# The state-space scan's 248 small operations, issued on GpSimd in place of VectorE

## The chip, the cores and the metric

The kernel runs on one core of a Trainium2 chip. The metric is the device time of one execution in microseconds (us). In the profile, PE is TensorE (matmul) and PEld its weight loads, DVE is VectorE, ACT is ScalarE, POOL is GpSimd, and SP is SyncE, which issues most DMAs. The span is the time from the first to the last instruction of the one execution that was profiled.

## The reference

The reference is one encoder layer over 512 tokens of width 1024. Two mixers run side by side, a state-space branch (S5) and a gated spatial branch (SGU), are merged by sigmoid gates, and are followed by cross-attention on 256 memory tokens and a SwiGLU network of width 2816. The part that matters here is the S5 branch:

```python
def s5_scan(u, lam_re, lam_im, log_step, b_re, b_im, c_re, c_im, reverse):
    ...
    lam_bar = jnp.exp(lam * step)
    ...
    bu = jnp.einsum('gpc,lbgc->lbgp', b_bar, u.astype(jnp.complex64))
    a = jnp.broadcast_to(lam_bar[None, None], (seq, 1) + lam_bar.shape)
    _, states = lax.associative_scan(_linear_recurrence, (a, bu), axis=0, reverse=reverse)
    ...
    return jnp.einsum('gcp,lbgp->lbgc', c, states).real

def s5_branch(xa, ...):
    ...
    for direction, reverse in ((0, False), (1, True)):
        y = y + s5_scan(...)
    y = jax.nn.gelu(y.transpose(1, 0, 2, 3).reshape(bsz, seq, S5_WIDTH))
    y = y * jax.nn.sigmoid(y @ w_glu.astype(f32))
    return y.astype(xa.dtype)
```

There are 32 groups of 64 complex states, and one scan forward and one backward over the 512 positions.

## The kernel before, in words

**Tiles and products.** All weights are float32. A product of float32 matrices is made of three passes (`mm3`): each operand is split into a high part `hi`, a cast to a shorter format on ScalarE (L85), and a low part `lo`, a subtraction on VectorE (L86). A block of weights (128 x 1024 elements) is loaded by SyncE into `wraw`, cast into `whi`, and subtracted into `wlo`. `next_w` begins loads three blocks ahead and splits two blocks ahead; `whi` and `wlo` have three buffers each. One block of `feat` is 24 matmuls of 512 columns.

**Order.** The kernel is written as one sequence, and a planner (`TileContext(nc, schedule_with_timeline_sim=True)`) orders the instructions of every engine before the run, by its own times and by the program's order. What `in_order` pins comes behind all that was written before it on its engine; what follows may still be put ahead of it. On the chip every engine takes its queue in order.

**The side program.** The S5 branch is a generator that runs beside the main sequence of products. Each `yield` names the time that the instructions since the last one are worth. `tick(us)`, called after each piece of TensorE work, gives the generator a credit of 0.8 of that time, and resumes it for as long as there is credit; `later(n, fn)` puts a piece of work n ticks of 5.2 us later. A `yield` also decides how far down the main sequence the following S5 work is written. `finish_side`, behind the product 6 of the second half of `w_proj_b`, writes whatever is left.

**The scan.** Sequence positions are taken in 64 chunks of 8. The state inputs of all chunks are in `zh` (128 partitions: 64 states forward and 64 backward; free: chunk, real and imaginary part, 32 groups). `s5_inputs` fills `zh` (matmuls `pz` L968, copies L973 on ScalarE and L974 on VectorE). `s5_scan` then goes through chunks 1 to 62, with four operations on 128 x 64 elements for each: two products with the constants `ca` and `cb` (L996, L997), and two additions (L998, L999). Each chunk needs the one before.

**After the scan.** For each of four parts o of eight groups, `s5_outputs` sets two edges of `ss` to zero on GpSimd (L1010, L1011), copies the states out of `zh`, one half on ScalarE (L1012) and one on VectorE (L1013), multiplies on TensorE (`py` L1025), copies (`yn` L1034), turns on TensorE (`pyt` L1040), and copies into `y` (L1045). Parts 2 and 3 must first load their factors again (`reload`, L943 and L936). `store_outputs`, called at three places between the products of `w_proj_b` and once behind `finish_side`, takes the parts that are there by then: a GELU on ScalarE (L1057) and two DMAs on GpSimd (`yd`, L1060). Then `ygt` is read back (L1366), split (L1372, L1373), and the GLU's product begins on TensorE.

**The main sequence beside it.** In this order: `feat` blocks of the gates a (`ga0` to `ga3`, two blocks each), `psv` (L1214), the blocks of `zu`, the gates b (`gb0` to `gb3`, L1289), and the products of `w_proj_b` in seven half-size products for each half of the columns: 1, 5, 2, 6 of the first half, 1 of the second, 7, 2 (second), 4, 6 (second); `finish_side`; then 3, 7, 5, 4, 3 and the GLU.

**GpSimd's other work.** It raises norms to a power (L1153, L516), and issues DMAs: `kd` (L921), and the additions onto `bsum`, `qsum` and `dsum` (L294), each behind a first DMA that SyncE issues (L293).

Of the kernel before, what the change touches and what calls it, by code (L numbers as in the profile page):

```python
# [12 lines left out]
ALU = mybir.AluOpType  # L13
# [39 lines left out]
def hybrid_layer_kernel(  # L53
# [8 lines left out]
    nc = tc.nc  # L62
# [630 lines left out]
    st = {}  # L693
    V = nc.vector
# [294 lines left out]
            later(1, lambda i=i, e=e: turn(i, e))  # L989

    def s5_scan():
        zh = st["zh"]
        for n in range(1, NCH - 1):
            a = s5p.tile([P, 2, G], F32, tag="sa", name="sa", bufs=2)
            b = s5p.tile([P, 2, G], F32, tag="sb", name="sb", bufs=2)
            V.tensor_tensor(a, zh[:, n - 1], st["ca"], ALU.mult)  # L996
            V.tensor_tensor(b, zh[:, n - 1, ::-1, :], st["cb"], ALU.mult)  # L997
            V.tensor_tensor(a, a, zh[:, n], ALU.add)  # L998
            V.tensor_tensor(zh[:, n], a, b, ALU.add)  # L999
            yield 0.8  # L1000

    def s5_outputs(o):
        gs = slice(o * GO, (o + 1) * GO)
# [58 lines left out]
    def s5_program():  # L1062
        yield from s5_setup()
        for o in (2, 3):
            yield from s5_kernels(o)
        while "u" not in st:
            yield None
        zh = s5p.tile([P, NCH, 2, G], F32, name="zh")
        st["zh"] = zh
        for o in range(NO):  # L1070
            yield from s5_inputs(o)
        for o in (0, 1):
            yield from s5_kernels(o)
        while st.get("nz", 0) < 2 * NO:
            yield None
        yield None
        yield from s5_scan()
        for _ in range(2):
            yield None
        for o in range(NO):  # L1080
            yield from s5_outputs(o)
# [949 lines left out]
```

## Time and profile before

| | |
|---|---|
| time, median of two runs | 861.31 us (860.77 to 861.85) |
| span of the profiled execution | 859.5 us |
| TensorE busy | 852.2 us, 99% |
| VectorE busy | 663.7 us, 77% |
| ScalarE busy | 465.9 us, 54% |
| GpSimd busy | 86.2 us, 10%, 119 instructions |
| chain that ended last | TensorE 98% |
| scan, first and last operation | 135.0 and 227.8 us |

The profiled execution's own time is its span, 859.5 us, and what lies around it; the median of the runs is 1.8 us above the span. A row of the timeline has the start, the duration, the engine, the line, the operation, what is written from what is read, the shapes, and in square brackets how long the engine was idle before it and what ended that. A row of the groups has a count, the busy time, the mean of one in ns, and the idle time before them. The rows of the waits have the total, the number of times and the longest one in us.

### The profile page before, as it was taken

What the parts mean: (1) busy time and instruction counts of PE and PEld (TensorE: products, weight loads), DVE (VectorE), ACT (ScalarE), POOL (GpSimd) and SP (SyncE); (2) the same over time, 40 slices, a digit from 0 to 9 for tenths busy, and PEclk for the clock granted to TensorE, in tenths of its full rate; (3) what the DMA queues carried; (4) which work ended last, traced back from release to release, by engine and by line L of the source; (5) the groups of instructions that cost most, each with busy time, mean ns of one, the idle gap of its engine ahead of it and who ended that gap; (6) DMA issues with size and microseconds to landing.
All of it is one profiled execution on the core that took longest, in us unless ns stands there. A gap on an engine that the chain in (4) does not pass through costs nothing.

```text
span 859.5 us, 14730 instructions
## 1 busy us (share of the span) xinstructions
PE 852.2 (99%) x5760; PEld 764.1 (89%) x5760; DVE 663.7 (77%) x1078; ACT 465.9 (54%) x698; POOL 86.2 (10%) x119
## 2 busy tenths in 40 slices
PE   9999999999999999999999999999999999999997
PEld 6888888888889988899899888999999999988886
DVE  7898898899646867678758656767877768899776
ACT  7834953244455534457557444645545554655674
POOL 0002101211021111010010001010211111000000
PEclk9999999999999999999999999999999999999999
DMA  9869666888575798635696555557899898366664
GB/s 270 229 229 252 143 171 160 227 212 203 138 221 162 250 321 260 213 110 196 215 275 169 133 152 143 147 176 180 206 242 234 209 230 219 96 186 203 200 192 164
DMA packets 116200, 170.61 MB, mean 198 GB/s; under 512 B 9489, under 2 KB 80801, under 8 KB 116002
## 3 DMA queue, kind: packets, MB, share of 16 engines
q1 hardware_dynamic: 95778, 140.51, 50.8%
q0 software_dynamic: 20064, 28.55, 20.3%
q8 instruction: 45, 0.74, 0.3%
q10 hardware_dynamic: 288, 0.61, 0.2%
q14 instruction: 25, 0.20, 0.1%
HBM read 160.75 MB, written 48.73 MB: 244 GB/s over the span
## 4 chain that ended last, share of the span: by engine, by line
PE 98%; DMA 1%; ACT 0%; SPq 0%; DVE 0%; issue 0%
PE pf L379 27%; PE pt L379 17%; PE px L1261 13%; PE pq L1261 6%; PE dx L379 5%; PE dq L379 5%; PE pv L1261 3%; PE bx L1261 3%; PE qx L1261 3%; PE dv L379 2%; PE pz L968 2%; PE qv L1261 1%; PE po L379 1%; PE psc L379 1%; PE py L1025 1%; PE qq L1261 1%
## 5 line engine op out<-in xcount | busy, mean ns | idle before, releaser
L85 ACT CAST whi<-wraw 128x1024 fp32r<-128x1024 f32 x141 | 145.3, 1031 | 161.4 <-PE pf L379 61.0
L86 DVE TENSOR_TENSOR wlo<-wraw,whi 128x1024 fp32r<-128x1024 f32 x141 | 168.2, 1195 | 55.5 <-ACT whi L85 54.8
L379 PE MATMUL pf<-xn,whi 128*128 128x512 f32 x448 | 139.4, 392 | 0.0
L379 PEld LDWEIGHTS pf<-xn,whi 128*128 128x128 f32 x448 | 83.4, 188 | 16.9 <-issue 0.2
L379 PE MATMUL pf<-xn,wlo 128*128 128x512 f32 x224 | 87.7, 392 | 0.0
L1261 PE MATMUL px<-fn,whi 128*128 128x256 f32 x480 | 83.5, 277 | 0.0
L1261 PEld LDWEIGHTS px<-fn,whi 128*128 128x128 f32 x480 | 72.5, 188 | 0.2
L86 DVE TENSOR_TENSOR wlo<-b,whi 128x1024 fp32r<-128x1024 f32 x40 | 48.9, 1223 | 26.0 <-ACT whi L85 26.0
L85 ACT CAST whi<-b 128x1024 fp32r<-128x1024 f32 x40 | 42.2, 1054 | 47.8 <-PE px L1261 27.8
L1261 PE MATMUL px<-fn,wlo 128*128 128x256 f32 x240 | 66.4, 277 | 0.0
L1261 PE MATMUL pq<-s,whi 128*128 128x256 f32 x320 | 55.0, 276 | 0.0
L86 DVE TENSOR_TENSOR wlo<-t,whi 128x1024 fp32r<-128x1024 f32 x30 | 36.7, 1225 | 19.4 <-ACT whi L85 19.4
L85 ACT CAST whi<-t 128x1024 fp32r<-128x1024 f32 x30 | 31.6, 1054 | 36.1 <-PE pv L1261 13.4
L379 PEld LDWEIGHTS pf<-xn,wlo 128*128 128x128 f32 x224 | 42.0, 188 | 8.9 <-issue 0.2
L1261 PEld LDWEIGHTS pq<-s,whi 128*128 128x128 f32 x320 | 48.1, 188 | 0.0
L1261 PEld LDWEIGHTS px<-fn,wlo 128*128 128x128 f32 x240 | 45.1, 188 | 0.0
L1261 PE MATMUL pq<-s,wlo 128*128 128x256 f32 x160 | 44.2, 276 | 0.0
L379 PE MATMUL pt<-whi,xn 128*128 128x512 f32 x128 | 43.4, 404 | 0.0
L379 PE MATMUL dx<-whi,s 128*128 128x512 f32 x132 | 41.4, 390 | 0.0
L379 PE MATMUL dq<-whi,s 128*128 128x512 f32 x122 | 38.1, 389 | 0.0
L294 POOL DMA_DIRECT2D dsum<-in_w_down_dram x12 | 13.3, 1105 | 170.4 <-DMA dsum<-in_w_down_dram 166.2
L1261 PEld LDWEIGHTS pq<-s,wlo 128*128 128x128 f32 x160 | 30.1, 188 | 0.0
(456 smaller groups left out, 2221.7 us busy)
## 6 DMA issues: line engine op xcount, KB each, us to landing
wraw<-in_w_in_dram SPq DMA_DIRECT2D x34, 512.0 KB, 5.2
dsum<-in_w_down_dram SPq DMA_DIRECT2D x20, 512.0 KB, 6.3
wraw<-dsum SPq DMA_DIRECT2D x20, 512.0 KB, 4.3
b<-in_w_gate_dram SPq DMA_DIRECT2D x15, 512.0 KB, 5.2
b<-in_w_up_dram SPq DMA_DIRECT2D x15, 512.0 KB, 5.4
wraw<-in_w_down_dram SPq DMA_DIRECT2D x15, 512.0 KB, 4.6
dsum<-in_w_down_dram POOLq DMA_DIRECT2D x10, 512.0 KB, 7.9
dsum<-dsum POOLq DMA_DIRECT2D x10, 512.0 KB, 7.9
```

Source lines behind the costliest of these rows:

```text
L85: hi = nc.scalar.copy(dst_hi, src)
L86: lo = nc.vector.tensor_tensor(dst_lo, src, dst_hi.bitcast(F32), ALU.subtract)
L294: plan[j + step][1].append((0, lambda d=dst, x=more: nc.gpsimd.dma_start(d, x, accum_op=ALU.add)))
L379: m = nc.tensor.matmul(ps, a[x], b[y], start=start and i == 0, stop=stop and i == 2, skip_group_check=free)
L968: nc.tensor.matmul(ps[:, g, :], wt[:, g, :], u[:, o * GO + g, :], start=True, stop=True)
L1025: in_order(nc.tensor.matmul(ps[64 * j:64 * j + 64, :, :, h, :].rearrange("p q d c -> p d q c"), a, b, start=k == ks[0], stop=k == ks[2], t ...
L1261: nc.tensor.matmul(ps[:, j, :], a[x], b[y], start=start and j == k == i == 0, stop=k == 3 and i == 2, skip_group_check=True)
```

## The change

The four operations of each chunk are issued on GpSimd (`nc.gpsimd`) where VectorE (`V`) had them, and the `yield` behind each chunk is 1.0 where it was 0.8. Nothing else differs.

```diff
     def s5_scan():
-        zh = st["zh"]
+        zh, S = st["zh"], nc.gpsimd
         for n in range(1, NCH - 1):
             a = s5p.tile([P, 2, G], F32, tag="sa", name="sa", bufs=2)
             b = s5p.tile([P, 2, G], F32, tag="sb", name="sb", bufs=2)
-            V.tensor_tensor(a, zh[:, n - 1], st["ca"], ALU.mult)
-            V.tensor_tensor(b, zh[:, n - 1, ::-1, :], st["cb"], ALU.mult)
-            V.tensor_tensor(a, a, zh[:, n], ALU.add)
-            V.tensor_tensor(zh[:, n], a, b, ALU.add)
-            yield 0.8
+            S.tensor_tensor(a, zh[:, n - 1], st["ca"], ALU.mult)
+            S.tensor_tensor(b, zh[:, n - 1, ::-1, :], st["cb"], ALU.mult)
+            S.tensor_tensor(a, a, zh[:, n], ALU.add)
+            S.tensor_tensor(zh[:, n], a, b, ALU.add)
+            yield 1.0
```

## The prediction

> **What bounds the kernel now.** I read the page's head first, then the waits of TensorE, then one stage.
>
> ```profile
> span 859.5 us, 14730 instructions
> PE 852.2 (99%) x5760; PEld 764.1 (89%) x5760; DVE 663.7 (77%) x1078; ACT 465.9 (54%) x698; POOL 86.2 (10%) x119
> ```
>
> The waits of TensorE in the whole run:
>
> ```profile
> PE pt L582 <- DVE ones L498: 1.1, 1, 1.1
> PE ptr L644 <- DVE xt L638: 0.3, 1, 0.3
> PE pt L379 <- DVE wlo L660: 0.3, 1, 0.3
> ```
>
> TensorE sets the time. It is busy for 852.2 of 859.5 us and waited 1.7 us in all, at the start. VectorE never holds it up afterwards, in the stage of the scan either:
>
> ```profile
> core 0: us, PE busy (x) PEld busy (x) DVE busy (x) ACT busy (x) POOL busy (x), PEclk, DMA share, GB/s
> 135.00:229.00 94.00, 94.00 (x567) 78.82 (x566) 84.90 (x312) 35.02 (x50) 13.15 (x16) 1.00 0.80 201
> 229.00:299.00 70.00, 70.00 (x627) 65.44 (x625) 42.39 (x53) 39.30 (x48) 13.18 (x25) 1.00 0.63 196
> ```
>
> TensorE is busy for all 94.00 us of the scan and all 70.00 us from there to the GLU, with VectorE at 84.90. So work taken off VectorE here can buy nothing by itself. The sum starts at the span, 859.5 us; the runs' median of 861.31 lies 1.8 us above it, which I add at the end.
>
> **What the change removes: nothing on the path.** One step on VectorE, from its timeline, and the scan's end:
>
> ```profile
> 135.04 0.23 DVE L996 TENSOR_TENSOR sa<-zh,ca 128x64 f32<-128x64 f32 x1
> ...
> 135.57 0.23 DVE L999 TENSOR_TENSOR zh<-sa,sb 128x64 f32<-128x64 f32 x1
> 135.83 0.23 DVE L996 TENSOR_TENSOR sa<-zh,ca 128x64 f32<-128x64 f32 x1
> ...
> 227.81 0.22 DVE L999 TENSOR_TENSOR zh<-sa,sb 128x64 f32<-128x64 f32 x1
> ```
>
> A step takes 0.79 us (135.04 to 135.83), 62 steps 49 us. They fill the gaps between the casts' subtractions and end at 228.03. All 49 us leave VectorE. TensorE is covered already, so I book 0; the 1.7 us of its waits is the most that could ever be gained.
>
> **What it adds: 248 two-input operations on GpSimd, a price that no row has.** The nearest rows of that engine, with what it issues in the stretch besides:
>
> ```profile
> 125.61 0.12 POOL L1010 MEMSET ss<- 64x16 f32 x1 [11.88 <-issue]
> 125.78 0.12 POOL L1011 MEMSET ss<- 64x16 f32 x1
> 353.61 0.55 POOL L516 TENSOR_TENSOR r<-ms,mhalf 128x1 f32<-128x1 f32 x1 [9.55 <-DVE ms L515]
> ...
> L294 POOL DMA_DIRECT2D qsum<-in_w_q_dram x6 | 6.9, 1156 | 53.1 <-DMA qsum<-in_w_q_dram 33.8 <-DMA qsum<-qsum 19.2
> L921 POOL DMA_DIRECT2D kd<-ks x8 | 3.9, 494 | 4.4 <-DVE zh L999 2.6 <-DVE sb L997 1.9
> L294 POOL DMA_DIRECT2D bsum<-in_w_proj_b_dram x2 | 2.3, 1169 | 17.3 <-DMA bsum<-bsum 17.3
> ```
>
> Below stands a memset, spaced 0.17 us (125.61 to 125.78), which reads nothing: 248 x 0.17 = 42 us. Above stands the same kind of instruction, two inputs, one element, but a power: 0.55 us, 248 x 0.55 = 136 us. A multiplication of 64 elements lies between; I take 0.35 us, the middle, as the form is the upper row's and the function the cheaper: 248 x 0.35 = 87 us. The 16 DMA issues of the stretch go through the same engine: 6.9 + 3.9 + 2.3 = 13 us.
>
> **A third term: both engines at SBUF.** One row shows GpSimd held up by VectorE:
>
> ```profile
> 236.35 1.06 DVE L1013 COPY ss<-zh 64x1008 f32<-64x1008 f32 x1 [1.22 <-PE py L1025]
> 236.47 1.00 POOL L1010 MEMSET ss<- 64x16 f32 x1 [15.36 <-PE py L1025]
> ```
>
> The memset that takes 0.12 us elsewhere took 1.00 us and ended at 237.47, just behind the copy's end at 237.41. The memset at 125.61 ran at 0.12 us while VectorE worked, but it reads nothing; no row has a GpSimd operation with SBUF inputs beside a VectorE operation with two of them. What of that sort stays on VectorE between 135 and 229:
>
> ```profile
> L86 DVE TENSOR_TENSOR wlo<-wraw,whi 128x1024 fp32r<-128x1024 f32 x15 | 18.3, 1223 | 4.2 <-ACT whi L85 4.2
> L1176 DVE SCALAR_TENSOR_TENSOR mix<-squares,gbc,mix 128x128 f32<-128x128 f32 x8 | 3.0, 453 | 0.0
> L1237 DVE TENSOR_TENSOR zf<-zf,sv 128x512 f32<-128x512 f32 x4 | 2.8, 689 | 0.4 <-ACT zf L1236 0.4
> ```
>
> These are 24.1 us; the zu product, L1245, L1299, L1300 and the yb_lo subtractions are of the same form and bring it to about 39 us. Bounds of the term: 0, and 39 us if GpSimd stands through all of it. I take 20, about half, since VectorE stops for part of the time in what follows. On VectorE's side each of its operations waits at most for one short one, which its freed 49 us cover; without that cover, TensorE would wait for wlo.
>
> So the scan starts where it does now, at 135, when the last zh copy is in, and **ends at 135 + 87 + 13 + 20 = 255 us instead of 228** (bounds 135 + 42 + 13 = 190 and 135 + 136 + 13 + 39 = 323).
>
> **Who waits for it.** What stands on ScalarE around the present end:
>
> ```profile
> 220.18 1.05 ACT L85 CAST whi<-wraw 128x1024 fp32r<-128x1024 f32 x1 [3.89 <-issue]
> 225.58 1.06 ACT L85 CAST whi<-wraw 128x1024 fp32r<-128x1024 f32 x1 [4.34 <-PE pf L379]
> 228.06 3.91 ACT L1012 COPY ss<-zh 64x1008 f32<-64x1008 f32 x2 [1.43 <-DVE zh L999]
> ```
>
> The ss copies stand in ScalarE's queue between two casts of weights, and their halves (L1013) in VectorE's between two subtractions. The queues are written before the run by a planner with times of its own, and nothing passes a waiting copy. For VectorE's scan it was right to 1.43 us. If it takes GpSimd for faster than it is, the copies stand too early, and the next casts stand behind them.
>
> Where it will put them I can only bound. By the code's own pacing, 1.0 per step now (0.8 stood for the measured 0.79), the scan would end at 135 + 62 + 13 = 210; with a right price at 255. I take 225, a third of the way, as the planner orders by prices and not by stands. Weights are split two blocks ahead, and a block lasts 5.40 us (220.18 to 225.58). So TensorE runs on for half a block and two more, 2.7 + 10.8 = 13.5 us, and is dry at 238.5. The scan ends at 255, two ss copies take 3.9 us, and at 259 TensorE gets work again (first py, then pf). **TensorE stands 259 - 238.5 = 20.5 us.** The clock row stays at 1.00.
>
> **What the pacing alone costs: 2 us.** A step's yield goes from 0.8 to 1.0: at the rate of 0.8 the scan takes 77.5 us of ticks in place of 62, three blocks of 5.2 more. I counted the ticks through the code. py of outputs 0 and 1 moves from the end of gb1 to gb3, py of 2 and 3 to behind the products 7 (first half) and 4, and both last pyt to behind the product 6 of the second half, into finish_side. The present chain from there:
>
> ```profile
> 274.06 0.60 PE L1040 MATMUL pyt<-ident,yn 128*128 128x128 f32 x4
> 274.70 0.69 DVE L1045 COPY y<-pyt 128x512 f32<-128x512 f32 x1 [0.96 <-PE pyt L1040]
> 263.56 1.28 ACT L1057 ACT_TABLE_LOAD   x1
> 278.28 0.63 ACT L1057 ACTIVATE y<-y 128x512 f32<-128x512 f32 x1
> 279.20 1.20 POOL L1060 DMA_DIRECT2D yd<-y  x2 [1.47 <-ACT y L1057]
> 285.20 2.25 POOL L1366 DMA_DIRECT2D ygt<-yd  x4 [0.33 <-issue]
> 292.58 2.19 ACT L1372 CAST yg_hi<-ygt 128x512 fp32r<-128x512 f32 x4
> 293.38 0.68 DVE L1373 TENSOR_TENSOR yg_lo<-ygt,yg_hi 128x512 fp32r<-128x512 f32 x1
> 299.00 0.39 PE L379 MATMUL pf<-yg_hi,whi 128*128 128x512 f32 x1
> yd<-y POOLq DMA_DIRECT2D x8, 128.0 KB, 3.8
> ygt<-yd POOLq DMA_DIRECT2D x4, 256.0 KB, 4.6
> ```
>
> On today's clock the GLU begins at 299, and the second half's product 6 ends near 285 (299 less five products, for which the code ticks 2.7 us each). Behind 285: two pyt 1.2, a copy 0.7, two gelus and the table load 2.5, four yd issues 2.4 and 3.8 to landing, the first ygt issue 0.6 and 4.6 to landing, cast and subtraction 1.3: 302 against 299 plus the 1.2 us of pyt that now lies behind 285. That is 2 us of standing, once, with bounds of 0 and 5; the five products between cover the rest.
>
> **Sum:** 859.5 + 20.5 + 2 = 882, and 1.8 around it: **884 us**, 2.6% above the median. Own range 868 to 900: 10 us to either side for where the copies are queued, 6 for the price.
>
> In a sentence that the sum does not need: the Trainium skill, "SBUF — State Buffer", section "SBUF: two separate sides", says that a VectorE instruction with two SBUF inputs and a GpSimd instruction that reads SBUF lock each other out for a whole instruction. The rows above agree for a copy and show nothing for this pair; by the rule the 20 us would be 39.
>
> **The rivals.** (a) *Not slower: the scan is there in time, or the queues know when it comes.* The point is where the copies end by 238.5: scan end 234.5, so (234.5 - 135 - 13) / 62 = 1.40 us per step or 0.35 us per operation, stands included. At 0.25 us without stands the scan ends at 210. The two memsets speak for it, the power row against. Only the pacing is left: 859.5 + 2 + 1.8 = 863. Where the planner prices it late but rightly, the GLU's chain is about 10 us later: 871.
>
> (b) *GpSimd stands through all of VectorE's two-input work.* The scan ends at 274, 19 us later: 903. For it speaks the memset of 1.00 us, against it that VectorE stops once the casts do. The rule just named is this rival.
>
> (c) *The operation costs what the power costs.* 136 in place of 87: 49 us more, 933. Against it: one element at 0.55 us must be mostly the power's own work.
>
> (d) *SyncE instead.* The kd issues (L921) queue behind scan operations, SyncE stands at the tt loads, and weight loads behind it come late. With three blocks of load lead, 16 us, a lag of some 10 us costs at most 5: 868.
>
> (e) *Faster by over 2%*: no row shows 17 us that VectorE costs TensorE.
>
> **How the numbers follow.** Forecast 0.50, (a) 0.26, (b) 0.14, (c) 0.05, (d) 0.03, (e) 0.02. Two per cent is 17 us, about what a measurement of this kernel can tell from no change: the line is 878.5 us. Some 0.08 of the forecast lies below it: slower 0.42 + 0.14 + 0.05 = 0.61, faster 0.02, within 0.37. The range of 862 to 908 takes in (b) and most of (a), and leaves (c) out.
>
> **What would show it.** Right: four-operation steps of 1.4 us or more on GpSimd, longer beside wlo; the scan's last operation near 255; ScalarE's ss copy with a wait of 20 us or more on GpSimd; casts behind it late; a hole in TensorE of some 20 us between 235 and 262; and a wait of about 2 us before the GLU. VectorE's busy time falls by about 50 us. Wrong: no hole, with the scan ended by 235 or the copies queued behind its end; or a hole in another place, such as before the weights of the zu stage.

## The result, and the profile after

The changed kernel takes **898.07 us** (median of two runs, 896.3 to 899.83) against 861.31: a ratio of 1.042, 95% interval 1.041 to 1.044. It is slower by 36.8 us; the profiled execution is the upper of the two runs, 1.7 us above its span. The forecast was 884, with a range of 862 to 908.

The head of the page after:

```profile
span 898.1 us, 14725 instructions
PE 860.9 (96%) x5760; PEld 769.5 (86%) x5760; DVE 627.0 (70%) x830; ACT 466.1 (52%) x698; POOL 184.3 (21%) x367
```

VectorE lost 248 instructions and 36.7 us of busy time, GpSimd gained both the instructions and 98.1 us. TensorE has the same 5760 matmuls and is busy for 8.7 us *longer*. Its longest waits:

```profile
PE py L1025 <- DVE ss L1013: 22.2, 1, 22.2
PE pf L379 <- ACT yg_hi L1372: 3.6, 2, 2.3
PE pf L379 <- ACT ya_hi L85: 3.2, 1, 3.2
```

Two places are new: one stand of 22.2 us for the states, and 6.8 us at the GLU. With the 8.7 us of longer matmuls they make 37.7 of the 38.6 us by which the span grew (859.5 to 898.1). By stage:

```profile
136.00:240.00 104.00, 104.00 (x611) 87.12 (x611) 49.01 (x65) 37.28 (x53) 88.48 (x192) 1.00 0.72 185
240.00:262.00 22.00, 5.18 (x23) 3.94 (x22) 0.06 (x1) 0.00 (x0) 19.56 (x63) 0.66 0.26 48
262.00:285.00 23.00, 17.61 (x167) 16.32 (x168) 13.49 (x18) 16.57 (x19) 8.37 (x23) 0.80 0.52 164
285.00:305.00 20.00, 20.00 (x197) 19.57 (x196) 13.12 (x15) 9.94 (x13) 2.48 (x4) 1.00 0.71 207
305.00:340.00 35.00, 31.43 (x237) 28.54 (x237) 18.02 (x22) 13.03 (x16) 6.00 (x10) 0.90 0.78 242
```

The columns are the window, its length, busy time of TensorE, weight loads, VectorE, ScalarE and GpSimd, the granted clock, the DMA share and GB/s. Up to 240 TensorE misses nothing. From 240 to 262 it has 5.18 us of work left, up to 245.2, and then only GpSimd works: ScalarE at 0.00, VectorE at 0.06. The granted clock is below 1.00 in the three windows that hold a stand of TensorE, and 1.00 in the one between them that holds none.

The scan itself, from GpSimd's timeline: its first operations, a step beside a long subtraction, and its end; and VectorE's subtraction of that moment:

```profile
136.44 0.32 POOL L996 TENSOR_TENSOR sa<-zh,ca 128x64 f32<-128x64 f32 x1 [1.96 <-DVE zh L974]
...
189.02 0.32 POOL L996 TENSOR_TENSOR sa<-zh,ca 128x64 f32<-128x64 f32 x1
189.30 0.33 POOL L997 TENSOR_TENSOR sb<-zh,cb 128x64 f32<-128x64 f32 x1
189.59 0.32 POOL L998 TENSOR_TENSOR sa<-sa,zh 128x64 f32<-128x64 f32 x1
189.99 1.33 POOL L999 TENSOR_TENSOR zh<-sa,sb 128x64 f32<-128x64 f32 x1
191.40 0.32 POOL L996 TENSOR_TENSOR sa<-zh,ca 128x64 f32<-128x64 f32 x1
```

```profile
189.91 1.23 DVE L86 TENSOR_TENSOR wlo<-wraw,whi 128x1024 fp32r<-128x1024 f32 x1 [1.16 <-ACT whi L85]
```

An operation of 0.32 us that started 0.08 us behind `wlo` took 1.33 us and ended at 191.32, 0.18 us behind the subtraction's end at 191.14. The subtraction took its usual time. GpSimd's transfers in the stretch, two of them with a stand for a landing:

```profile
162.72 1.21 POOL L294 DMA_DIRECT2D bsum<-in_w_proj_b_dram  x1 [4.66 <-DMA bsum<-bsum]
167.81 1.18 POOL L294 DMA_DIRECT2D qsum<-in_w_q_dram  x1 [3.54 <-DMA qsum<-in_w_q_dram]
```

And who waited, on ScalarE, for an end of the scan at 265.4:

```profile
237.74 1.06 ACT L85 CAST whi<-wraw 128x1024 fp32r<-128x1024 f32 x1 [4.38 <-PE pf L379]
265.45 1.89 ACT L1012 COPY ss<-zh 64x1008 f32<-64x1008 f32 x1 [26.65 <-POOL zh L999]
```

The copy was queued behind the cast of 237.7 and stood there for 26.65 us, with every later cast behind it. On TensorE the last `pf` block ended at 245.2, and the first `py` came at 267.4.

Out of these rows the scan's 129 us (136.4 to 265.4) come apart as follows. Steps with nothing beside them are 1.36 us apart, and 62 of them are 84.3 us. The issues of the 16 transfers are 13.3 us. The two stands for landings are 8.2 us. The remaining 23 us is what the operations took longer beside VectorE. This last item was a remainder so far, and the theory for it was one of two. **Contention theory:** operations of GpSimd that read SBUF stand while VectorE runs one with two SBUF inputs. **Rival:** the scan is late by its own operations and its queue, and the long rows are chance. For the time lost by the lateness the theory was that only the end of the scan counts, against the time that its readers are queued for; its rivals were the pacing, and GpSimd's work as such.

### The profile page after: what moved, and what is told of

Same layout as the page of the kernel before. It is cut to its first block, busy times and chain, and to the rows that moved or that the text cites. A ratio compares the mean times of both kernels' runs of the same rounds, so it can differ in the third digit from the quotient of the medians.

```text
span 898.1 us, 14725 instructions
## 1 busy us (share of the span) xinstructions
PE 860.9 (96%) x5760; PEld 769.5 (86%) x5760; DVE 627.0 (70%) x830; ACT 466.1 (52%) x698; POOL 184.3 (21%) x367
## 4 chain that ended last, share of the span: by engine, by line
PE 80%; POOL 12%; DMA 4%; issue 1%; ACT 1%; DVE 1%; SPq 1%; POOLq 0%
PE pt L379 16%; PE pf L379 15%; PE px L1261 12%; PE pq L1261 6%; PE dx L379 5%; PE dq L379 5%; POOL zh L999 3%; PE pv L1261 3%; POOL sa L996 3%; POOL sa L998 3%; PE qx L1261 2%; POOL sb L997 2%; PE dv L379 2%; PE bx L1261 2%; PE pz L968 2%
## 5 line engine op out<-in xcount | busy, mean ns | idle before, releaser
L86 DVE TENSOR_TENSOR wlo<-b,whi 128x1024 fp32r<-128x1024 f32 x40 | 48.9, 1223 | 25.7 <-ACT whi L85 25.7
L86 DVE TENSOR_TENSOR wlo<-t,whi 128x1024 fp32r<-128x1024 f32 x30 | 36.7, 1225 | 19.6 <-ACT whi L85 19.6
L294 POOL DMA_DIRECT2D dsum<-in_w_down_dram x12 | 13.3, 1106 | 168.6 <-DMA dsum<-in_w_down_dram 164.8
L1025 PE MATMUL py<-e,ss 128*64 128x128 f32 x128 | 11.2, 302 | 22.2 <-DVE ss L1013 22.2
```

What stands on the lines that cost most here:

```text
L86: lo = nc.vector.tensor_tensor(dst_lo, src, dst_hi.bitcast(F32), ALU.subtract)
L294: plan[j + step][1].append((0, lambda d=dst, x=more: nc.gpsimd.dma_start(d, x, accum_op=ALU.add)))
L1025: in_order(nc.tensor.matmul(ps[64 * j:64 * j + 64, :, :, h, :].rearrange("p q d c -> p d q c"), a, b, start=k == ks[0], stop=k == ks[2], t ...
```

## The experiments

The runs of the kernel before that stand beside them had medians of 861.85 us (the first four experiments), 862.12 (the next three) and 861.92 (the last two).

### The pacing alone

The scan stays on VectorE, only the `yield` changes:

```diff
-            yield 0.8
+            yield 1.0
```

> The scan stays on VectorE, only its yield is 1.0. Queue theory (the time is lost because the copies out of zh stand in ScalarE's and VectorE's queues ahead of weight casts, earlier than GpSimd's scan ends): the scan ends near 228 us as before, no hole of TensorE at py; only the shorter way to the GLU is left, some 2 to 7 us: 863 to 868 us. Pacing rival (the later place of the outputs is the cause): most of the 37 us is here, 885 to 898 us.

Measured: 873.39 us, ratio 1.013 (1.0115 to 1.0145). This is between the two expectations, and far above the 2 us that the prediction gave it. Its waits, and the chain in front of the GLU:

```profile
PE pf L379 <- ACT yg_hi L1372: 3.9, 2, 2.3
PE pf L379 <- ACT ya_hi L85: 3.2, 1, 3.2
```

```profile
289.98 0.63 ACT L1057 ACTIVATE y<-y 128x512 f32<-128x512 f32 x1 [0.41 <-DVE y L1045]
290.91 1.20 POOL L1060 DMA_DIRECT2D yd<-y  x2 [1.61 <-ACT y L1057]
296.69 0.14 POOL L137 MEMSET pad<- 128x48 f32 x1 [4.58 <-DMA yd<-y]
297.16 2.24 POOL L1366 DMA_DIRECT2D ygt<-yd  x4 [0.33 <-issue]
301.49 0.62 ACT L1372 CAST yg_hi<-ygt 128x512 fp32r<-128x512 f32 x1 [3.34 <-DMA ygt<-yd]
304.78 0.62 ACT L1372 CAST yg_hi<-ygt 128x512 fp32r<-128x512 f32 x1 [2.67 <-DMA ygt<-yd]
```

The last GELU ran at 278.28 in the kernel before and runs at 289.98 here, though the scan is as early as ever: the larger `yield` writes the readers of `ss` further down the sequence. The GLU keeps its place. So `yd` is issued 11.7 us later, `ygt` 12.0 us later (285.20 to 297.16), and the GLU's first products stand for the read-back, 7.1 us, the same as in the kernel after (6.8). TensorE's matmuls take 3.2 us longer on top (852.2 to 855.4 busy). The 11.5 us (873.39 less 861.85) belong to the pacing, and none of it to GpSimd.

### The scan on GpSimd without the pacing

The change with `yield 0.8` kept.

> The scan on GpSimd with the old yield of 0.8. In its ScalarE queue 34 casts of weights stand ahead of the first copy out of zh, where the changed kernel has 36. Queue theory: two casts fewer ahead make the hole of TensorE about 11 us longer (22 to 33 us), and the way to the GLU is longer again, less 2 to 7 us: 901 to 908 us. Pacing rival: the pacing is that of before, so 861 to 865 us. Lateness rival (what is lost is GpSimd's lateness of 37 us itself, wherever the copies stand): 894 to 898 us.

Measured: 888.59 us, ratio 1.031 (1.029 to 1.033). All three expectations missed. One late wait is left, and the place of the copies is again behind a cast at 237.7:

```profile
PE py L1025 <- DVE ss L1013: 24.4, 1, 24.4
```

The two waits at the GLU are gone. The copies were not queued earlier than in the kernel after, though the `yield` is smaller, so it isn't the `yield` that places them; a price of the planner's own for the scan, with an end near 240 in either kernel, would fit, but no run shows that price. What the pacing adds to the move is 9.5 us (898.07 less 888.59), close to the 11.5 that it costs alone.

### Later readers

The `ss` copies pinned in program order, and written four ticks later, with `yield 1.0`:

```diff
+        in_order(nc.scalar.copy(...))          # ss, L1012
+        in_order(V.tensor_copy(...))           # ss, L1013
...
-        for _ in range(2):
+        for _ in range(6):
             yield None
```

> The scan on GpSimd with yield 1.0; the copies out of zh are pinned in program order and written four ticks later, so that 39 casts of weights stand ahead of the first in ScalarE's queue in place of 36. Queue theory: TensorE has about 11 to 16 us more work ahead of py; its hole of 22 us falls to 0 to 8 us, and a wait before the GLU grows to 5 to 12 us since all that follows is later: 868 to 882 us, though the scan ends as late as in the changed kernel (265 us). Lateness rival: 895 to 900 us. Pacing rival: later pacing makes it worse, above 900 us.

Measured: 896.12 us, ratio 1.039 (1.037 to 1.042). The number is the one of the lateness rival, and the hole of the queue theory, 0 to 8 us, did not come out.

```profile
PE qv L1261 <- ACT qv L1274: 18.8, 1, 18.8
PE pf L379 <- ACT ya_hi L85: 3.2, 1, 3.2
PE pf L379 <- ACT yg_hi L1372: 3.1, 2, 2.4
```

The copies still stood for 17.7 us, and the wait only moved: casts and evictions behind them came late, so TensorE stood for `qv` in place of `py`. The scan ended 4 us later than in the kernel after (269.6). By the same subtraction as above its contention is 27 us where the kernel after has 23, as VectorE went on with its subtractions beside it, and its stands for landings are 10.0 us where that has 8.2. To queue the readers behind the scan's real end isn't free either, as the first experiment showed for the GLU.

### The first 16 chunks alone

```diff
         for n in range(1, NCH - 1):
+            S = nc.gpsimd if n <= 16 else V
...
             yield 0.8
```

> Only the first 16 of the 62 chunks run on GpSimd, the others on VectorE, yield 0.8. Queue theory: GpSimd has them done within some 35 us (16 steps of 1.36 us, DMA issues and stands between), VectorE does the other 46 in 36 us of its gaps, and the scan still ends near 228 to 235 us with the copies behind 34 casts: 860 to 866 us, no gain from the 13 us taken off VectorE. If work on GpSimd beside VectorE costs TensorE time by itself, a quarter of the 37 us: 870 us. If VectorE's freed time were worth something: below 858 us.

Measured: 861.60 us, ratio 1.000 (0.999 to 1.001). The scan ended later than expected, and nothing waited for it:

```profile
237.70 1.05 ACT L85 CAST whi<-wraw 128x1024 fp32r<-128x1024 f32 x1 [4.38 <-PE pf L379]
240.60 3.93 ACT L1013 COPY ss<-zh 64x1008 f32<-64x1008 f32 x2 [1.84 <-DVE zh L1000]
```

Here the copies stand behind a cast at the same 237.70 and wait 1.84 us. So an end at 240.5, 12 us later than before, costs nothing, and operations on GpSimd cost nothing as such. VectorE's 10.9 us of relief (663.7 to 652.8 busy) bought nothing.

### VectorE calmed

On the kernel of the second experiment, the low part of the weight blocks that are split during the scan is set by a memset (it is left out of the product), in place of a subtraction with two SBUF inputs:

```diff
+        if place is None and 18 <= len(tiles) <= 36:
+            cast[0] = nc.scalar.copy(hi, src)
+            nc.vector.memset(lo.bitcast(F32), 0.0)
+            return hi, lo
         cast[0] = split(hi, lo, src)
```

> The scan on GpSimd, pacing 0.8 as in e2_gpsimd_yield_08, and for the weight blocks that are split while the scan runs the low part of the weights is set by a memset in place of the two-input subtraction (leaves out the low part of these weights), so that VectorE does some 20 us less of two-input work between SBUF operands in that stretch; every instruction keeps its engine and place. Contention theory: the excess of the scan's operations over 0.32 us each (22.6 us in the kernel after) falls to 8 to 12, the scan ends at 252 to 255 in place of 265, the wait of TensorE for ss falls from 24.4 to 10 to 14, time 873 to 877. Rival, the scan is late by its own operations and by what GpSimd's queue waits for: the end moves by under 4 us, wait 21 to 24, time 886 to 889.

Measured: 876.43 us, ratio 1.017 (1.015 to 1.018). The contention theory's numbers came out: the scan ended at 252.3, and the wait halved.

```profile
PE py L1029 <- DVE ss L1017: 12.0, 1, 12.0
```

A memset of VectorE, and GpSimd's operations beside it (lines are shifted by 4 in this kernel):

```profile
220.75 0.91 DVE L114 MEMSET wlo<- 128x1024 f32 x1 [4.53 <-PE pf L383]
```

```profile
220.88 0.32 POOL L1003 TENSOR_TENSOR zh<-sa,sb 128x64 f32<-128x64 f32 x1
221.28 0.32 POOL L1000 TENSOR_TENSOR sa<-zh,ca 128x64 f32<-128x64 f32 x1
221.55 0.33 POOL L1001 TENSOR_TENSOR sb<-zh,cb 128x64 f32<-128x64 f32 x1
```

The memset lasts 0.91 us where the subtraction lasts 1.22, writes the same tile, and holds nobody up. The timeline's 248 operations can be sorted by what ran on VectorE beside them. In this kernel 47 ran beside such a memset, with a mean of 0.35 us; in the kernel after, 25 ran beside `wlo` subtractions, with a mean of 0.95 us and up to 1.39, and one of 1.72 whose row also overlaps the issue of a transfer. The scan's 117.0 us here, less 84.3, 13.3 and 10.2 of stands for landings, leave 9 us of contention where the kernel after has 23. Most of the rest falls beside the two-input operations on `zu`, `zf` and `yb_lo`, which this kernel keeps.

### Six transfers taken out of the stretch

On the kernel of the second experiment the places in the plan of six `qsum` transfers are moved out of the stretch, and with them those of two `bsum` transfers, which come 4 places earlier (18 and 20 in place of 22 and 24):

```diff
-    ... [(18 + 2 * i, 3) for i in range(8)] +
+    ... [(37, 3), (39, 3), (18, 3), (20, 3), (41, 3), (43, 3), (45, 3), (47, 3)] +
```

With these places a sum of `w_proj_b` is begun before the sum that it builds on has its last term, so these weights have other values; the amount of work is the same.

> The scan on GpSimd, pacing 0.8, and six of the qsum transfers that GpSimd issues between the steps of the scan are given to it before or after that stretch. Theory that the queue's transfers count in full: 6 issues at 1.15 us and the 3.5 us stand for a landing leave the scan, it ends about 10 us earlier (254 to 256), the wait for ss falls to 14 to 18 (the copies themselves may be planned some 3.6 us earlier), time 878 to 883. Rival, the contention simply falls on other operations and the order of the work takes back what the scan gains, since the copies are queued earlier too: wait 21 to 24, time 885 to 889.

Measured: 893.70 us, ratio 1.036 (1.035 to 1.038): 5 us more than the kernel it starts from, worse than either expectation. The scan did end earlier, at 260.6, but by 5 us instead of 10. The issues fell from 13.3 to 7.6 us only, as three `bsum` transfers are in the stretch where two were, and the stands for landings rose from 8.8 to 11.6. The planner queued the copies one cast earlier, and the wait was as long as ever:

```profile
PE py L1025 <- DVE ss L1013: 23.6, 1, 23.6
PE bx L1261 <- ACT u L1279: 4.3, 1, 4.3
```

```profile
231.50 1.06 ACT L85 CAST whi<-wraw 128x1024 fp32r<-128x1024 f32 x1 [4.38 <-PE pf L379]
260.58 3.76 ACT L1012 COPY ss<-zh 64x1008 f32<-64x1008 f32 x2 [28.02 <-POOL zh L999]
...
322.69 1.04 ACT L85 CAST whi<-wraw 128x1024 fp32r<-128x1024 f32 x1 [7.28 <-DMA wraw<-in_w_proj_b_dram]
```

The last row is behind the second wait: a cast stood 7.28 us for its weights, and the copy `u` behind it came 4.3 us late for TensorE. So the 5 us more are not the scan's, and this run speaks of the scan by its first wait alone, 23.6 against 24.4. There an earlier end was worth nothing, since the readers' place moved with it: what the planner had counted it takes back. The lateness would then be what it hadn't counted, the contention and the stands; that is not shown.

### The first 32 chunks

As the 16 chunks, with `n <= 32`.

> The first 32 chunks on GpSimd, the other 30 on VectorE, pacing 0.8; the copies of ss are queued where e2_gpsimd_yield_08 and e4_first_16_chunks have them. In the kernel after, chunk 32 ended at 216. Theory that only the end of the scan against about 240 counts: VectorE does the other 30 at 0.8 to 1.2 us each and ends at 240 to 252; wait of TensorE 0 to 11 us; time 862 to 872, the span longer than that of e4 by that wait and up to 4 us for a slower clock behind it. Rival, each chunk on GpSimd costs its part of the 27 us wherever the scan ends: 32/62 of it, 875 with the wait at 12 or more.

Measured: 868.63 us, ratio 1.008 (1.006 to 1.009). The number lies in the first theory's interval, but the wait isn't where that put it:

```profile
PE pf L379 <- DVE wlo L86: 6.2, 1, 6.2
```

```profile
DVE sa L997 <- POOL zh L1000: 15.3, 1, 15.3
```

At the handover VectorE stood for 15.3 us for GpSimd's 32nd chunk, and a `wlo` behind that in its queue came 6.2 us late for TensorE. The span is 7.9 us above that of the 16 chunks (868.6 against 860.7), of which this wait is 6.2. VectorE then did its 30 steps in time: the scan ended at 248.0, and the copies waited 1.28 us, behind a cast of 245.7. So one cost turned into another: late steps in one engine's queue cost there, at whatever point another engine meets them.

### The form of the subtraction, and its size

One group of rows of the kernel after spoke against a stand beside any two SBUF inputs. Eight operations of VectorE on 128 x 128 with two such inputs, and GpSimd's timeline beside them:

```profile
141.96 3.03 DVE L1176 SCALAR_TENSOR_TENSOR mix<-squares,gbc,mix 128x128 f32<-128x128 f32 x8
```

```profile
142.17 0.38 POOL L998 TENSOR_TENSOR sa<-sa,zh 128x64 f32<-128x64 f32 x1
142.62 0.32 POOL L999 TENSOR_TENSOR zh<-sa,sb 128x64 f32<-128x64 f32 x1
143.03 0.32 POOL L996 TENSOR_TENSOR sa<-zh,ca 128x64 f32<-128x64 f32 x1
```

Nothing there took over 0.38 us. Either the form or the size may let GpSimd through. Two kernels part them. Both compute the low part in full, for the same blocks as above; the first with the form of `mix` in the old size, the second with the old form in eight pieces:

```diff
-            nc.vector.memset(lo.bitcast(F32), 0.0)
+            nc.vector.scalar_tensor_tensor(lo, hi.bitcast(F32), -1.0, src, ALU.mult, ALU.add)
```

> As e5_calm_vector, but the low part of the weight blocks split during the scan is computed in full, by a scalar_tensor_tensor (whi times -1 plus wraw) in place of a tensor_tensor: the same two SBUF inputs, the same size, the same output. In the kernel after, eight scalar_tensor_tensor of 128x128 (L1176, 0.45 us each, two SBUF inputs) ran beside GpSimd's operations and none of these took over 0.38 us. Theory that two SBUF inputs are what holds GpSimd up, whatever the form: its operations beside these subtractions take 0.9 us in the mean and up to 1.7 us, scan end 262 to 267, time 885 to 890. Rival, the form decides, and a scalar_tensor_tensor leaves GpSimd its port: mean 0.35 us beside them, scan end 250 to 254, wait of TensorE 10 to 14 us, time 873 to 878 as with the memset.

```diff
-            nc.vector.memset(lo.bitcast(F32), 0.0)
+            for j in range(k):
+                for c in range(0, n, 128):
+                    nc.vector.tensor_tensor(lo[:, j, c:c + 128], src[:, j, c:c + 128],
+                                            hi.bitcast(F32)[:, j, c:c + 128], ALU.subtract)
```

> As e9_scalar_tensor, but with tensor_tensor in eight pieces of 128x128 for each of these blocks. Theory that a tensor_tensor with two SBUF inputs holds GpSimd up for one instruction at a time: GpSimd gets its turn between pieces, no operation beside them takes over 0.32 + 0.3 us or so, but there are more of them; the sum of the delays falls, if turns alternate, to a half or less; scan end 252 to 260, time 876 to 884. Rival, pieces issued back to back hold the port as one: operations of up to 1.3 to 1.7 us again, scan end 262 to 267, time 885 to 890.

Measured: 888.55 us for the form, ratio 1.031 (1.029 to 1.032), and 882.19 us for the pieces, ratio 1.024 (1.022 to 1.026). The form changes nothing: 24 operations of GpSimd beside it took 0.94 us in the mean and up to 1.41 (1.75 with the issue of a transfer in the row), the scan ended at 264.6, and TensorE waited as long as ever:

```profile
PE py L1029 <- DVE ss L1017: 24.3, 1, 24.3
```

The pieces let GpSimd take turns, though VectorE needs twice the time for them, 2.35 us for eight:

```profile
216.99 2.35 DVE L116 TENSOR_TENSOR wlo<-wraw,whi 128x128 fp32r<-128x128 f32 x8 [1.47 <-ACT whi L113]
```

```profile
217.06 0.40 POOL L1005 TENSOR_TENSOR sa<-sa,zh 128x64 f32<-128x64 f32 x1
217.54 0.45 POOL L1006 TENSOR_TENSOR zh<-sa,sb 128x64 f32<-128x64 f32 x1
218.07 0.46 POOL L1003 TENSOR_TENSOR sa<-zh,ca 128x64 f32<-128x64 f32 x1
```

Beside the pieces 84 operations took 0.42 us in the mean, 80 of them at most 0.47. The scan ended at 258.8: its 122.5 us less 84.3, 13.3 and 10.3 leave 15 us of contention, the wait fell to 17.6 us. So what GpSimd loses is at most the length of one VectorE instruction at a time, and a long instruction costs it most. The contention theory holds: the memset, the pieces and the full subtraction leave 9, 15 and 23 us of contention, waits of 12.0, 17.6 and 24.4 us, and times of 876.4, 882.2 and 888.6 us.

## Why the prediction was right or wrong

The direction, the mechanism and the place were right; the size was 14 us short. Step by step:

- **VectorE's freed time is worth nothing: right.** The 16 chunks showed it, at a ratio of 1.000.
- **0.35 us an operation: right.** Uncontended steps are 1.36 us apart, 0.34 an operation, 84.3 us where 87 were booked. The power row was indeed the far bound.
- **13 us of issues: right** (13.3). **What hangs on them was left out:** the engine that runs the scan also stands until the first half of a sum has landed, 4.66 and 3.54 us. The prediction quoted rows with such idle times, 53.1 and 17.3 us of them, and booked nothing for them. In a queue that carries the critical chain they are part of its length.
- **Contention 20 us: right in kind, and near in size** (23 as a remainder, of which 14 went with the subtractions of the weights alone). Rival (b), a stand through all 39 us, put the scan's end at 274; it was 265. The Trainium skill, "SBUF — State Buffer", section "SBUF: two separate sides", has the two engines lock each other out, for the whole instruction of whichever starts first. The rows agree, the 1.33 us beside a `wlo` of 1.23 and the memset that delays nothing among them. The size matters with it, since GpSimd loses one instruction at a time: the 3.0 us of `mix`, which the prediction counted into its 39, cost GpSimd next to nothing. Why they cost even less than the pieces of the same size (at most 0.38 us an operation against 0.42 in the mean) stays open.
- **The scan's end at 255: 10 us early**, the stands for landings 8.2, the start 1.4 us later, and 3 more of contention against 3 less for the price.
- **The queue as if for 225, TensorE dry at 238.5: too early.** The copies stood behind a cast at 237.7, and TensorE ran dry at 245.2. The scan's end was late by more than that, and the hole of 20.5 us, measured at 22.2, was close partly by luck: two errors of 7 to 10 us had the same sign.
- **"The clock row stays at 1.00": wrong.** It fell to 0.66 and 0.80 around the hole and to 0.90 around the GLU, and the 5760 matmuls took 8.7 us longer, of which 3.2 appear with the pacing alone. This is the largest part missing from the sum. The three stretches of the kernel after in which the granted clock was 0.50:

```profile
247.24:271.13 23.89, 3.74 (x36) 3.74 (x38) 1.97 (x3) 5.62 (x5) 16.06 (x54) 0.50 0.12 19
329.16:335.98 6.82, 5.60 (x13) 4.14 (x13) 4.23 (x6) 3.89 (x5) 1.23 (x1) 0.50 1.10 267
346.22:349.64 3.42, 3.42 (x8) 2.74 (x9) 3.42 (x6) 1.04 (x2) 0.00 (x0) 0.50 0.91 232
```

TensorE was busy for 12.8 us of them, which at half the clock is 6.4 us more than at the full one, an estimate from these rows, out of the 8.7. The first stretch goes on for 3.7 us behind the first `py` of 267.4. The Trainium skill, "TensorE: Matmul & The Clock Gate", section "Part 1: The HAM clock gate", has the array fall to half its rate after an idle window of about 3.4 us. The trace agrees on the half, 0.50, but not on the time: the clock fell at 247.24, 2.1 us after TensorE ran dry.

- **2 us for the pacing, bounds 0 to 5: mis-sized.** The chain was worked out nearly to the point: the working had the first `yg` tile ready at 302, and with the pacing alone its cast ended at 302.1. What was missing lies behind it. The working let the rest follow without a stand, but the next tile's read-back landed late, ScalarE stood 2.67 us for it until 304.78, and `ya_hi` came 3.2 us late after that. This last stand is also one of order: in the kernel before, the first output of the GLU was read (L1386) at 302.84, 3.8 us after its first product at 299.00, and with the pacing alone at 313.95, 11.8 us after the first at 302.17, as the products of the outputs were queued side by side. The stands were 7.1 us alone and 6.8 in the kernel after; in time the pacing was worth 11.5 and 9.5 us.

Against the profiled execution, 899.8 us, the sum of 884 lacks 15.8: 1.7 of hole, 4.8 at the GLU (6.8 less 2), 8.7 of longer matmuls, and 0.6 that is left for small waits.

What stays open: the 2.3 us of longer matmuls that the half clock does not cover. The 16 chunks, without any stand and at a full clock, have 853.8 us of busy time, 1.6 over the kernel before, so that some of it does not come from stands. How the planner places the readers of the scan is not shown either. A version in which the planner prices the scan rightly and the GLU is moved back with it was not tried. No version here was faster than the kernel before.

## What to carry to other kernels

An operation that moves to an idle engine takes on that engine's queue: the transfers that it issues, the landings that it stands for, and what it loses beside another engine. The price per operation, right here to 3%, accounts for 84 of the scan's 129 us. Cost it against the time for which its readers are queued, which is read on the waiting engine: an end up to 240 cost nothing here, and one 25 us later cost 27. Pacing that orders other work is a change of its own, to be costed apart; it was a quarter of the loss. And a stand of the engine that sets the time costs more than its length, by the slower clock behind it.

## What the runs showed of the hardware

- A GpSimd operation on 128 x 64 float32 with two SBUF inputs takes 0.32 us, and four that depend on one another 1.36 us. VectorE takes 0.22 us for the same, and 0.79.
- Beside VectorE instructions with two SBUF inputs it stands for the rest of the instruction: up to 1.39 us beside 1.22 us of 128 x 1024, 0.42 in the mean beside pieces of 128 x 128. VectorE pays little: its `wlo` mean between 136 and 266 went from 1223 to 1268 ns.
- Behind a stand of TensorE the granted clock was still 0.50 for some us of work, and for not much longer after a long stand than after a short one: TensorE was busy at 0.50 for 5.1 us behind a stand of 6.2 (the first 32 chunks), 4.9 behind 12.0 (the memset), 4.9 behind 17.6 (the pieces) and 4.6 behind 24.4 (the second experiment). In all the runs it was 2.9 to 5.8 us behind the stand at the scan. At half the clock that is 1.4 to 2.9 us on top of the length of the stand, an estimate from these figures.
- The stands at the GLU, none over 3.2 us, brought the clock to 0.50 as well, in 329.2 to 336.0 and 346.2 to 349.6 of the kernel after.
